# A diffusion step on one Trainium2 core: a fifth unit of the modulation summed on VectorE in the first mixer, begun a quarter of the in-projection earlier, and one narrower widened matmul per head in the second mixer

## The chip, the cores and the metric

The program runs on one core of a Trainium2 chip. The core has a TensorE (matrix products; PE in the profile, its weight loads PEld), a VectorE (DVE), a ScalarE (ACT), a GpSimd (POOL) and a SyncE (SP), which here issues nearly all DMA transfers. Each engine runs its own list of instructions in order, and the engines wait for each other through semaphores. The metric is device time in microseconds (us), as a median of runs; smaller is better.

## What is computed

One step of a diffusion backbone with two layers, for 128 context tokens and 128 latent tokens that share all weights, with D = 2048 features, in 32 bit floating point:

```python
def _trunk(x, cond, rope, caches, w_ada, b_ada, ...):
    for l in range(DEPTH):
        mod = jax.nn.silu(cond) @ w_ada[l] + b_ada[l]
        sh1, sc1, gt1, sh2, sc2, gt2 = jnp.split(mod[:, None, :], 6, axis=-1)
        h = rmsnorm(x, g_norm_mix[l]) * (1 + sc1) + sh1
        ...
            m, new = mixer_ab(h, rope, ctx, w_in_ab[i], ...)
        ...
            m, new = mixer_c(h, rope, ctx, l, w_in_c[i], ...)
        x = x + gt1 * m
        h = rmsnorm(x, g_norm_ffn[l]) * (1 + sc2) + sh2
        x = x + gt2 * conv_ffn(h, w_ffn_up[l], w_ffn_conv[l], b_ffn_conv[l], w_ffn_down[l])
    return rmsnorm(x, g_final), ab_ctx, c_ctx

def mixer_ab(h, rope, ctx, w_in, g_q, w_q_up, g_kv, w_kv_up, g_qn, g_kn, w_out):
    proj = h @ w_in
    ...
    out = jnp.concatenate([out_a.reshape(b, t, -1), out_b.reshape(b, t, -1)], axis=-1) @ w_out
    return out, new_ctx
```

`mixer_ab`, the first mixer, has eight heads of latent attention and eight of grouped attention; `mixer_c`, the second, is differential attention. The modulation `mod` has six vectors of 2048 numbers for each layer and each of the two conditions (`c_ctx` and `c`). Its matrix `w_ada` is 2 x 2048 x 12288 numbers, 201 MB of the 617 MB that the program moves.

## The kernel before

**The products.** Activations stand with features on partitions: `hx[:, k]` holds row k, 128 features by 256 columns (both groups' tokens), as a high half in 256 columns and a low half in the next 256. A weight tile of 1 MB is split into a high part `wh` (ScalarE, L248) and a low part `wl` (VectorE, L249), eight 128 x 128 blocks at a time. Each block then takes three matmuls of 256 columns (L110): high by high, high by low, low by high; I call these three a triplet. `wh` and `wl` have four buffers each, which the splits take in turn. TensorE adds in PSUM into tiles named `acc`.

**The in-projection of the first mixer** runs over 23 chunks (c0 to c22) of 128 output features. It passes over them five times, each time with a part of the 16 rows: `whole` (rows 0, 1), `halves` (2, 3), quarter 1 (rows 4 to 7), quarter 2 (8 to 11) and the last quarter (12 to 15). In the three quarters a chunk takes 12 matmuls. After a chunk VectorE adds its sum to the ones before (L1143). Up to the end of quarter 2, the order of TensorE's instructions is that of the program (`pe.in_turn`); in the rest a scheduler sorts each engine's list by a timeline that it simulates, and `keep_order` holds chosen instructions in the order of the program. What the list then says is fixed: on the chip an engine doesn't run a later instruction first.

**The modulation** is worked out beside these products, in units (l, j, q): layer, vector (0 to 5) and quarter of 512 features. A unit has four tiles of 1 MB (128 x 2048 numbers). There are three ways to make one. A *row unit* (`ROWS`) takes TensorE: 16 matmuls of 32 x 512 for two tiles, a *pair*, and four transposes per unit (L113), then a reduce (L445) and an addition of the bias (L447) on VectorE. A *feature unit* (`FEATS`) is summed on VectorE in the feed-forward layers. A *deep unit* (`DEEP`, class `Deep`) is summed on VectorE in the mixers: each tile comes in two halves of 512 KB (L522), one for each half of the 2048 inputs, and for each half-tile there are two sums, one for each condition (L525; in the trace a custom instruction and a read of its accumulator). A unit has 16 such sums. They need the row `condb` of the conditions, loaded a half (1 MB, L513) at a time and passed through SiLU by ScalarE (L516). `deep.pump` is called after every chunk and takes as many steps as `deep.rate` says, 0.4 a chunk in the last quarter and 1.6 a call in the heads.

**In quarters 1 and 2**, `quarter(q)` says what is done after which chunk: pairs of row units after c4, c8, c13 and c17, the transposes of the first unit after c10, and after c19 those of the second, which complete shift and scale of the next quarter's four rows. Then `rows(q + 1)` calls `modulate`: VectorE scales the four rows (L658, one of the groups) and ScalarE the other group; ScalarE casts the high halves; the low halves come from VectorE for the even rows (L647) and from GpSimd for the odd ones. After c22 the next quarter begins at once with these rows.

**The second mixer** has a matmul with a widened operand at two of 13 places per head, so as to shift the matmuls' rhythm: `PUSH` gives the extra columns. The first is the one that follows the scores, the last the one that follows the head's output.

Of the kernel before, what the change touches and what calls it, by code (L numbers as in the profile page):

```python
# [58 lines left out]

EARLY = (2, 5, 8, 11, 13)  # L60
WIDER = (32, 16, 8, 4, 2)
PUSH = [32] + 11 * [0] + [16]
SENT = (1, 3, 6, 9, 12, 14, 16)
FINE = 4

# [9 lines left out]


ROWS = [(0, j, q) for q in range(4) for j in (1, 0)]
ROWS += [(0, j, q) for j in (2, 4) for q in range(4)]
ROWS += [(0, 5, 0)]
ROWS += [(1, 2, 1), (1, 2, 2), (1, 2, 3), (1, 4, 0), (1, 3, 0)]  # L80
FEATS = [(0, 5, 1), (0, 5, 2), (0, 5, 3)]
FEATS += [(1, j, q) for j in (1, 0) for q in range(4)]
FEATS += [(1, 2, 0)]
FEATS += [(1, 5, q) for q in range(4)]
DEEP = [[(0, 3, q) for q in range(4)], [(1, 4, q) for q in range(1, 4)] + [(1, 3, q) for q in range(1, 4)]]
RLIMIT = {"ab": 16, "ffn0": 17, "c": 22, "ffn1": 22}
FLIMIT = {"ab": 0, "ffn0": 12, "c": 12, "ffn1": 16}

SIDE = {"in3": 0.4, "heads": 1.6, "out0": 1.8, "c": 2.2, "outc": 2.0}
UW = NT + 2  # L90
INV = {2048: 0, 768: 1, 512: 2, 128: 3, 256: 4}

# [2 lines left out]
def step_kernel(ctx: ExitStack, tc: tile.TileContext, A: dict):  # L95
# [96 lines left out]
    def flush():  # L192
        while chains:
            step()
# [299 lines left out]
    class Deep:  # L494
# [50 lines left out]

        def flush(self):
            while self.steps:
                self.step()

    deep = Deep()  # L550
# [366 lines left out]
    def mixer_ab(hx, beside):  # L917
        l = 0
        with tc.tile_pool(name="ab", bufs=1) as ab:
            with tc.tile_pool(name="abp", bufs=1) as pj:  # L920
# [187 lines left out]
                def values(c):  # L1108
                    pt = T_(ppool["att"], [P, 512], "att", bufs=3)
                    for g in range(2):  # L1110
                        pe.transpose(pt[:, g * T:(g + 1) * T], vb[:, c, g * T:(g + 1) * T], ident)
                    act.copy(vg[:, 0, c], pt[:, 0:T])
                    act.copy(vg[:, 2, c], pt[:, T:NT])
                    if c == 1:
                        sp.dma_start(out=A["o_gqa_v"], in_=vg[:, 0])
                    yield

                def finish(c):
                    if c == 7:
                        deep.silu()  # L1120
                        deep.rate = SIDE["in3"]
                    if c < 6:
                        start(queries(c))
                    elif c < 10:
                        start(latents(c - 6))
                    elif c == 10:
                        start(key_rope())
                    elif c < 13:
                        start(keys(c - 11))
                    elif c == 14:  # L1130
                        start(values(0))
                    elif c == 15:
                        start(values(1))
# [60 lines left out]

                def quarter(q):
                    u = 2 * q + 2
                    return {4: lambda: pair(u, 0), 8: lambda: pair(u, 2), 10: turned, 13: lambda: pair(u + 1, 0),
                            17: lambda: pair(u + 1, 2), 19: lambda: turned(q + 1)}

                def at(steps):  # L1200
                    return lambda c: steps[c]() if c in steps else None
# [3 lines left out]
                for q in (1, 2):  # L1205
# [3 lines left out]
                kv_in = T_(ab, [P, 4, 2, 3 * T], "kv_in", F32R)  # L1209
                ql = T_(ab, [P, 6, 2 * NT], "ql", F32R)  # L1210
                caches()
                deep.begin(beside, DEEP[0], [(beside, "block")],
                           mod[:, 0, 5].rearrange("p (i t) c -> p i t c", t=4), hx[:, 0:2])
                deep.cond(0)
                part(rest, 12, 4, False, RATE["in3"], finish)

            with tc.tile_pool(name="abh", bufs=1) as hp:
                ada["pew"] = PEW["heads"]
# [59 lines left out]
                flush()  # L1278
                weigh_lambda()
                start(gqa_query(0))  # L1280
                deep.tiles.append((ab, "kvb"))
                deep.junk = o[:, 6:8]
                deep.rate = SIDE["heads"]
                for h in range(0, 8, 2):
                    for i in range(2):
                        ps = gemm(WQ.chunk(), qh, qlo)
                        qn[h + i] = T_(hp, [P, NT], "qn", bufs=4)
                        act.copy(qn[h + i], ps)
                        pump(RATE["heads"])
                    ps = gemm(WQ.chunk(), qh, qlo)  # L1290
                    ev = T_(tmp, [P, NT], "nt", bufs=4)
                    act.copy(ev, ps)
                    qr = T_(hp, [P, NT], "qr", bufs=2)
                    act.copy(qr[:, 0:T], ev[:, 0:T])
                    rope(qr[:, None, T:], ev[:, None, T:], 1, 32, "rcm", "rsm")
                    pump(RATE["heads"])
                    kn = []
                    for i in range(2):
                        if h + i < 7:
                            start(gqa_query(h + i + 1))  # L1300
                        start(gqa(h + i))
                        ps = gemm(WK.chunk(), kh, klo, 3 * T)
                        kn.append(T_(hp, [P, 3 * T], "kn", bufs=2))
                        act.copy(kn[i], ps)
                        pump(RATE["heads"])
                    mla_pair(h, qr, kn, values())
                flush()

        return o
# [471 lines left out]
```

## Time and profile before

| what | us |
|---|---|
| median of 3 runs (lowest, highest) | 2304.95 (2304.35, 2306.54) |
| the profiled execution | 2307.52 |
| its span | 2305.7 |
| `whole` and `halves` of the in-projection | 26 to 84 |
| quarter 1, quarter 2 | 84 to 126, 126 to 167 |
| last quarter, then the heads (they overlap) | 167 to about 205, to 355 |
| output projection of the first mixer | 355 to 475 |
| first feed-forward layer | 475 to 1166 |
| second mixer with its output projection | 1192 to about 1512 |
| second feed-forward layer | 1580 to 2306 |

All times in views of the profile are microseconds from the start of the span. A row of the timeline gives start, duration, engine, line, operation, the tiles written and read, and, in brackets, idle time before it and what ended that; the recorded durations of neighbours overlap a little, so that the step from one start to the next is the time that one takes in a row of them. In the chain of waits a piece is a stretch on one engine that ended last.

### The profile page before, as it was taken

What the parts mean: (1) busy time and instruction counts of PE and PEld (TensorE: products, weight loads), DVE (VectorE), ACT (ScalarE), POOL (GpSimd) and SP (SyncE); (2) the same over time, 40 slices, a digit from 0 to 9 for tenths busy, and PEclk for the clock granted to TensorE, in tenths of its full rate; (3) what the DMA queues carried; (4) which work ended last, traced back from release to release, by engine and by line L of the source; (5) the groups of instructions that cost most, each with busy time, mean ns of one, the idle gap of its engine ahead of it and who ended that gap; (6) DMA issues with size and microseconds to landing.
All of it is one profiled execution on the core that took longest, in us unless ns stands there. A gap on an engine that the chain in (4) does not pass through costs nothing.

```text
span 2305.7 us, 47484 instructions
## 1 busy us (share of the span) xinstructions
PE 2275.9 (99%) x19496; PEld 2182.1 (95%) x19496; DVE 1885.6 (82%) x2973; ACT 1195.7 (52%) x1959; POOL 188.1 (8%) x238
## 2 busy tenths in 40 slices
PE   8999999999999999999999999999999999999998
PEld 6788878999999999999999999999999999999998
DVE  4667979989999999999978988898899965666654
ACT  4345555665553355555575455457555434555543
POOL 0002111300000000001130001023000000000011
PEclk9999999999999999999999999999999999999999
DMA  9987888777777777777788888776667755555553
GB/s 376 367 343 293 326 311 338 288 277 264 262 255 291 291 272 260 272 258 258 288 293 293 318 322 310 267 268 229 246 256 262 264 200 189 199 191 194 198 189 126
DMA packets 100122, 617.15 MB, mean 268 GB/s; under 512 B 10752, under 2 KB 18880, under 8 KB 33344
## 3 DMA queue, kind: packets, MB, share of 16 engines
q1 hardware_dynamic: 99904, 614.11, 72.2%
q8 instruction: 153, 2.51, 0.4%
q14 instruction: 65, 0.53, 0.1%
HBM read 609.32 MB, written 4.75 MB: 266 GB/s over the span
## 4 chain that ended last, share of the span: by engine, by line
PE 93%; DVE 3%; DMA 2%; issue 1%; POOL 1%; ACT 1%; SPq 0%; DVEq 0%; ACTq 0%; POOLq 0%
PE acc L110 86%; PE ada L110 3%; PE att L110 2%; DVE wl L249 1%; DVE hx L525 1%; DMA more<-w_ada 1%; PE att L113 1%; DMA raw<-w_out_c 0%; PE misc L110 0%; DMA araw<-w_ada 0%; DMA kvb<-w_ada 0%; POOL dev L807 0%; PE ada L113 0%; DVE rope L858 0%; ACT wh L248 0%
## 5 line engine op out<-in xcount | busy, mean ns | idle before, releaser
L110 PE MATMUL acc<-hx,wh 128*128 128x256 f32 (+1 forms) x7264 | 1255.2, 278 | 4.2 <-ACT wh L248 1.7
L248 ACT CAST wh<-raw 128x1024 fp32r<-128x1024 f32 (+1 forms) x834 | 796.6, 967 | 869.8 <-PE acc L110 736.6
L249 DVE TENSOR_TENSOR wl<-raw,wh 128x1024 fp32r<-128x1024 f32 (+1 forms) x834 | 925.4, 1126 | 246.9 <-ACT wh L248 240.2
L110 PEld LDWEIGHTS acc<-hx,wh 128*128 128x128 f32 x7264 | 1099.8, 188 | 23.2 <-ACT wh L248 8.1
L110 PE MATMUL acc<-hx,wl 128*128 128x256 f32 (+1 forms) x3632 | 1007.8, 278 | 5.3 <-DVE wl L249 5.1
L110 PEld LDWEIGHTS acc<-hx,wl 128*128 128x128 f32 x3632 | 684.5, 188 | 9.5 <-DVE wl L249 6.9
L110 PE MATMUL acc<-g,wh 128*128 128x256 f32 x2816 | 478.8, 276 | 0.0
L110 PEld LDWEIGHTS acc<-g,wh 128*128 128x128 f32 x2816 | 424.0, 188 | 0.0
L110 PE MATMUL acc<-g,wl 128*128 128x256 f32 x1408 | 388.1, 276 | 0.0
L473 DVE CUSTOM_DVE_ANT_0 junk<-araw,condb 128x2048 f32<-128x2048 f32 x128 | 294.4, 2300 | 0.0
L110 PEld LDWEIGHTS acc<-g,wl 128*128 128x128 f32 x1408 | 264.2, 188 | 0.0
L211 POOL TENSOR_TENSOR sqacc<-sqacc,sq 128x256 f32<-128x256 f32 x62 | 71.5, 1154 | 1491.1 <-ACT sq L207 1490.9
L110 PE MATMUL acc<-hxc,wh 128*128 128x256 f32 (+1 forms) x1056 | 189.3, 281 | 0.0
L110 PEld LDWEIGHTS acc<-hxc,wh 128*128 128x128 f32 x1056 | 161.9, 188 | 1.8 <-issue 1.7
L110 PE MATMUL acc<-hxc,wl 128*128 128x256 f32 (+1 forms) x528 | 146.9, 278 | 0.0
L110 PEld LDWEIGHTS acc<-hxc,wl 128*128 128x128 f32 x528 | 99.6, 189 | 0.2
L110 PE MATMUL acc<-wh,hxc 128*128 128x256 f32 (+1 forms) x512 | 95.0, 283 | 0.5 <-DVE nt L818 0.5
L1531 ACT ACTIVATE cv<-acc,convw 128x256 f32<-128x256 f32 x169 | 94.1, 557 | 0.0
L525 DVE CUSTOM_DVE_ANT_0 hx<-block,condb 128x1024 fp32r<-128x1024 f32 x65 | 79.3, 1221 | 7.3 <-DMA block<-w_ada 6.8
L1537 DVE SCALAR_TENSOR_TENSOR cv<-acc,convw,cv 128x254 f32<-128x254 f32 x169 | 81.1, 480 | 3.2
L843 DVE SCALAR_TENSOR_TENSOR x<-acc,mod,x 128x128 f32<-128x128 f32 x190 | 57.3, 344 | 31.6 <-PE acc L110 31.6
L110 PEld LDWEIGHTS acc<-wh,hxc 128*128 128x128 f32 x512 | 79.4, 188 | 3.4 <-issue 2.5
(263 smaller groups left out, 1800.4 us busy)
## 6 DMA issues: line engine op xcount, KB each, us to landing
raw<-w_up SPq DMA_DIRECT2D x176, 1024.0 KB, 4.8
araw<-w_ada SPq DMA_DIRECT2D x136, 1024.0 KB, 6.0
raw<-w_down SPq DMA_DIRECT2D x88, 1024.0 KB, 4.8
raw<-w_in_c SPq DMA_DIRECT2D x48, 1024.0 KB, 6.9
block<-w_ada SPq DMA_DIRECT2D x41, 512.0 KB, 6.8
raw<-w_in_ab SPq DMA_DIRECT2D x18, 1024.0 KB, 9.1
raw<-w_out_ab SPq DMA_DIRECT2D x16, 1024.0 KB, 7.9
raw<-w_out_c SPq DMA_DIRECT2D x16, 1024.0 KB, 7.1
```

The costliest lines, as they stand in the source:

```text
L110: return self.placed(nc.tensor.matmul(*a, **kw))
L113: return self.placed(nc.tensor.transpose(*a, **kw))
L211: eng.tensor_tensor(out=st["acc"], in0=st["acc"], in1=sq, op=ALU.add)
L248: pin(act.copy(out_hi, src))
L249: pin(dve.tensor_tensor(out=out_lo, in0=src, in1=out_hi.bitcast(F32), op=ALU.subtract))
L473: keep_order(dve.tensor_tensor_reduce(out=T_(feat["pool"], [P, D], "junk"), in1=feat["row"][:, c], in0=feat["raw"].rearrange("p g n -> p ( ...
L525: keep_order(dve.tensor_tensor_reduce(out=self.junk, in0=self.raw, in1=self.row[:, c].rearrange("p (g n) -> p g n", g=2), scale=1.0, scala ...
L843: dve.scalar_tensor_tensor(out=x[:, c, s], in0=ps[:, s], scalar=mod[:, l, 3 * which + 2, c, g:g + 1], in1=x[:, c, s], op0=ALU.mult, op1=AL ...
L1531: pin(act.activation(y, ps, AF.Identity, scale=cw[:, 1, m:m + 1], bias=cw[:, 3, m:m + 1]))
L1537: pin(dve.scalar_tensor_tensor(out=y3[:, :, :T - 1], in0=p3[:, :, 1:], scalar=cw[:, 2, m:m + 1], in1=y3[:, :, :T - 1], op0=ALU.mult, op1=A ...
```

## The change

`DEEP[0]` gets a fifth unit, (0, 4, 3), which leaves `ROWS`; so the first mixer and the first output projection make seven row units of vectors 2 and 4 where they made eight, and the limits `RLIMIT` fall by one. The deep sums no longer begin in the last quarter but with quarter 1: `begin_sums` loads the first half of `condb` after its chunk c0, `sums_ready` passes it through SiLU after c6 and sets the rate of 0.4. In the in-projection their tiles are `block` and `more` in turn, in the heads `block` and `kvb` as before. `deep.even()` takes a second condition's sum that is still due at the end of the last quarter and of the heads. The first of the two places in `PUSH` gets 16 extra columns instead of 32.

```diff
-PUSH = [32] + 11 * [0] + [16]
+PUSH = [16] + 11 * [0] + [16]
...
-ROWS += [(0, j, q) for j in (2, 4) for q in range(4)]
+ROWS += [(0, j, q) for j in (2, 4) for q in range(4)][:7]
...
-DEEP = [[(0, 3, q) for q in range(4)], [(1, 4, q) for q in range(1, 4)] + [(1, 3, q) for q in range(1, 4)]]
-RLIMIT = {"ab": 16, "ffn0": 17, "c": 22, "ffn1": 22}
+DEEP = [[(0, 4, 3)] + [(0, 3, q) for q in range(4)], [(1, 4, q) for q in range(1, 4)] + [(1, 3, q) for q in range(1, 4)]]
+RLIMIT = {"ab": 15, "ffn0": 16, "c": 21, "ffn1": 21}
...
-SIDE = {"in3": 0.4, "heads": 1.6, "out0": 1.8, "c": 2.2, "outc": 2.0}
+SIDE = {"in": 0.4, "in3": 0.4, "heads": 1.6, "out0": 1.8, "c": 2.2, "outc": 2.0}
...
+        def even(self):
+            while isinstance(self.steps[0], partial) and self.steps[0].func == self.sums and self.steps[0].args[-1]:
                 self.step()
...
                 def finish(c):
-                    if c == 7:
-                        deep.silu()
-                        deep.rate = SIDE["in3"]
...
                 def quarter(q):
                     u = 2 * q + 2
-                    return {4: lambda: pair(u, 0), 8: lambda: pair(u, 2), 10: turned, 13: lambda: pair(u + 1, 0),
-                            17: lambda: pair(u + 1, 2), 19: lambda: turned(q + 1)}
+                    steps = {4: lambda: pair(u, 0), 8: lambda: pair(u, 2), 10: turned, 13: lambda: pair(u + 1, 0),
+                             17: lambda: pair(u + 1, 2), 19: lambda: turned(q + 1)}
+                    return {**steps, 0: begin_sums, 6: sums_ready} if q == 1 else steps
+
+                def begin_sums():
+                    deep.begin(beside, DEEP[0], [(beside, "block"), (pj, "more")],
+                               mod[:, 1, 4:6].rearrange("p j (i t) c -> p (j i) t c", t=4), hx[:, 0:2])
+                    deep.cond(0)
+
+                def sums_ready():
+                    deep.silu()
+                    deep.rate = SIDE["in"]
...
                 caches()
-                deep.begin(beside, DEEP[0], [(beside, "block")],
-                           mod[:, 0, 5].rearrange("p (i t) c -> p i t c", t=4), hx[:, 0:2])
-                deep.cond(0)
+                deep.rate = SIDE["in3"]
                 part(rest, 12, 4, False, RATE["in3"], finish)
+                deep.even()
...
-                deep.tiles.append((ab, "kvb"))
+                deep.tiles = [(beside, "block"), (ab, "kvb")]
...
+                deep.even()
                 flush()
```

Counted over the lists, the sums of the first mixer rise from 64 to 80: in the in-projection, up to the last add of the last quarter, from 2 to 20 (4 in quarter 1, 8 in quarter 2, 8 in the last), in the heads from 44 to 42, in the output projection from 20 to 16. The removed row unit's two pairs and four transposes stood in the output projection. The loads of the caches move from quarter 2 to the last quarter. From the second mixer on TensorE's list is as before, apart from the widths. Lines behind the new `even` have numbers higher by four: L647, L658 and L951 become L651, L662 and L955; L1143 becomes L1144.

What moved on VectorE at the end of quarter 1 (`acc_1222` is chunk c19, the two acc behind it are c20 and c21; `nt_1243` and `nt_1255` are rows 8 and 10 being made), before:

```order
L1143 TENSOR_TENSOR qb_242<-qb_242,acc_1222 128x256
L445 TENSOR_REDUCE mod_77<-ada_1236 128x8
L447 TENSOR_TENSOR mod_77<-mod_77,cst_74 128x8
L658 TENSOR_SCALAR nt_1243<-nt_1243,scl_78,mod_77 128x128
L658 TENSOR_SCALAR nt_1249<-nt_1249,scl_78,mod_77 128x128
L658 TENSOR_SCALAR nt_1255<-nt_1255,scl_78,mod_77 128x128
L658 TENSOR_SCALAR nt_1261<-nt_1261,scl_78,mod_77 128x128
L249 TENSOR_TENSOR wl_1328<-raw_1089,wh_1327 128x1024
L1143 TENSOR_TENSOR qb_242<-qb_242,acc_1281 128x256
L647 TENSOR_TENSOR hx_104<-nt_1243,hx_104 128x256
L1143 TENSOR_TENSOR qb_242<-qb_242,acc_1295 128x256
L647 TENSOR_TENSOR hx_104<-nt_1255,hx_104 128x256
```

And in the change, from the add of chunk c19 (`acc_1236`) on; `nt_1257` is row 8, `raw_1096` and `raw_1175` are the first two weight tiles of quarter 2, `block_1135` a half-tile of a deep unit:

```order
L1144 TENSOR_TENSOR qb_242<-qb_242,acc_1236 128x256
L445 TENSOR_REDUCE mod_77<-ada_1250 128x8
L249 TENSOR_TENSOR wl_1339<-raw_1096,wh_1338 128x1024
L525 ISA hx_104,mod_77<-block_1135,condb_872 128x1024
L525 ISA mod_77 128x1
L447 TENSOR_TENSOR mod_77<-mod_77,cst_74 128x8
L249 TENSOR_TENSOR wl_1343<-raw_1096,wh_1342 128x1024
L1144 TENSOR_TENSOR qb_242<-qb_242,acc_1295 128x256
L1144 TENSOR_TENSOR qb_242<-qb_242,acc_1310 128x256
L525 ISA hx_104,mod_77<-block_1135,condb_872 128x1024
```

```order
L662 TENSOR_SCALAR nt_1275<-nt_1275,scl_78,mod_77 128x128
L1144 TENSOR_TENSOR qb_242<-qb_242,acc_1324 128x256
L249 TENSOR_TENSOR wl_1409<-raw_1175,wh_1408 128x1024
L249 TENSOR_TENSOR wl_1413<-raw_1175,wh_1412 128x1024
L651 TENSOR_TENSOR hx_104<-nt_1257,hx_104 128x256
L651 TENSOR_TENSOR hx_104<-nt_1269,hx_104 128x256
```

Between the two pieces stand the sum's second row and the other three scalings. Ahead of the first, from the add of chunk c17 on, stand a whole and a half weight low of `raw_1030`, the last tile of quarter 1, two sums on `more_1034` and the add of c18. So between the add of c17 and row 8's low half there are now six adds, five whole and one half weight low and four sums. `wh_1412` takes the buffer of `wh_1285`, which chunk c22 of quarter 1 reads, and ScalarE's list has the casts `wh_1408` and `wh_1412` ahead of the cast of row 8's high half.

VectorE at the end of quarter 2, in the change, from the add of c22 (`acc_1806`) on; `nt_1743` and `nt_1755` are rows 12 and 14, `raw_1927` the second weight tile of the last quarter, `acc_1837` its chunk c0:

```order
L1144 TENSOR_TENSOR qb_242<-qb_242,acc_1806 128x256
L651 TENSOR_TENSOR hx_104<-nt_1743,hx_104 128x256
L525 ISA hx_104,mod_77<-more_1658,condb_872 128x1024
L525 ISA mod_77 128x1
L249 TENSOR_TENSOR wl_1930<-raw_1927,wh_1929 128x1024
L525 ISA hx_104,mod_77<-more_1658,condb_872 128x1024
L525 ISA mod_77 128x1
L249 TENSOR_TENSOR wl_1934<-raw_1927,wh_1933 128x1024
L651 TENSOR_TENSOR hx_104<-nt_1755,hx_104 128x256
L1144 TENSOR_TENSOR proj_124<-proj_124,acc_1837 128x256
```

Before, one add stood between the two low halves. Now two sums and two weight lows stand there. From the add of c17 to row 12's low half there are six adds, three whole and one half weight low and two sums (on `block_1565`).

TensorE at the start of the last quarter, in the change; `acc_1837`, `acc_1859` and `acc_1882` are chunks c0, c1 and c2, `wh` and `wl` the parts of the weights; the sixth and the ninth row read row 13, the others row 12:

```order
L110 MATMUL acc_1837<-hx_104,wh_1829 128x256
L110 MATMUL acc_1859<-hx_104,wh_1829 128x256
L110 MATMUL acc_1882<-hx_104,wh_1833 128x256
L110 MATMUL acc_1837<-hx_104,wh_1829 128x256
L110 MATMUL acc_1837<-hx_104,wl_1830 128x256
L110 MATMUL acc_1837<-hx_104,wh_1829 128x256
L110 MATMUL acc_1859<-hx_104,wh_1829 128x256
L110 MATMUL acc_1859<-hx_104,wl_1830 128x256
L110 MATMUL acc_1859<-hx_104,wh_1829 128x256
```

The fourth row is the first that reads a low half of row 12. In the same manner row 13 follows for the three chunks, then row 14's high half for each, and the 22nd matmul is the first that reads row 14's low half. Before, the list here had chunks c0 and c1 in turn.

More of the change, by code (lines that the diff above doesn't have):

```diff
@@ L547, in flush @@
             while self.steps:
+                self.step()
+        def even(self):
+            while isinstance(self.steps[0], partial) and self.steps[0].func == self.sums and self.steps[0].args[-1]:
                 self.step()
```

## The prediction

> **What bounds the kernel now.** I read the chain of waits on the page first, to learn which engine sets the end, then the windows over the first mixer, then the chain and the VectorE timeline at the one place where the change is densest. The span and the chain:
>
> ```profile
> span 2305.7 us, 47484 instructions
> PE 93%; DVE 3%; DMA 2%; issue 1%; POOL 1%; ACT 1%; SPq 0%; DVEq 0%; ACTq 0%; POOLq 0%
> ```
>
> TensorE carries 93% of the chain, so an edit counts by the TensorE work it removes and by the waits it puts ahead of TensorE. The windows (stretch in us; its length, then busy time of PE, PEld, DVE, ACT, POOL; clock; DMA share; GB/s) are: whole and halves, quarter 1, quarter 2, most of the last quarter, the last heads, a piece of these, and the first half of the output projection:
>
> ```profile
> 26.00:84.00 58.00, 51.66 (x425) 41.60 (x425) 33.62 (x84) 27.67 (x58) 0.00 (x0) 0.94 0.97 401
> 84.00:126.00 42.00, 42.00 (x344) 35.73 (x344) 26.74 (x49) 15.42 (x23) 1.63 (x2) 0.96 0.87 350
> 126.00:167.00 41.00, 41.00 (x350) 34.73 (x349) 26.79 (x52) 16.31 (x24) 1.55 (x2) 1.00 0.87 343
> 167.00:205.00 38.00, 38.00 (x312) 32.88 (x312) 30.71 (x67) 25.04 (x54) 10.12 (x12) 1.00 0.73 276
> 300.00:355.00 55.00, 49.23 (x355) 38.41 (x354) 38.44 (x103) 29.03 (x70) 8.88 (x16) 0.94 0.72 277
> 326.00:336.00 10.00, 5.25 (x24) 1.60 (x23) 8.38 (x25) 2.56 (x9) 1.84 (x4) 0.70 0.74 269
> 355.00:415.00 60.00, 59.89 (x511) 53.05 (x509) 58.01 (x106) 32.68 (x58) 11.07 (x10) 1.00 0.94 366
> ```
>
> In both quarters TensorE never idles, and VectorE is idle for 42.00 - 26.74 = 15.3 us and 14.2 us. A share says nothing of order, though: VectorE runs its list strictly, and at a quarter's end that list holds the activation rows with which the next quarter begins.
>
> The chain at the two ends of quarters (start us, us, what):
>
> ```profile
> 116.24 1.85 PE ada L110 x16
> 118.09 2.95 PE acc L110 x24
> 121.48 11.31 PE acc L110 x96
> ...
> 157.42 1.85 PE ada L110 x16
> 159.27 2.95 PE acc L110 x24
> 162.66 14.98 PE acc L110 x132
> ```
>
> Chunk 17 ends at 116.24, a pair of row-unit tiles follows, then chunks 18 and 19, the transposes, and from 121.48 eight chunks without a gap: three of quarter 1 and, from 121.48 + 3/8 x 11.31 = 125.72, quarter 2. There the second matmul needs the low half of row 8, at 125.72 + 11.31/96 = 125.84. VectorE at that time (start, us, operation):
>
> ```profile
> 116.28 0.42 DVE L1143 TENSOR_TENSOR qb<-qb,acc 128x256 f32<-128x256 f32 x1 [0.34 <-PE acc L110]
> ...
> 121.52 0.19 DVE L445 TENSOR_REDUCE mod<-ada 128x8 f32<-128x32 f32 x1
> 121.74 0.17 DVE L447 TENSOR_TENSOR mod<-mod,cst 128x8 f32<-128x8 f32 x1
> 121.95 1.11 DVE L658 TENSOR_SCALAR nt<-nt,scl,mod 128x128 f32<-128x128 f32 x4
> 122.98 1.22 DVE L249 TENSOR_TENSOR wl<-raw,wh 128x1024 fp32r<-128x1024 f32 x1
> 124.11 0.41 DVE L1143 TENSOR_TENSOR qb<-qb,acc 128x256 f32<-128x256 f32 x1
> 124.44 0.86 DVE L647 TENSOR_TENSOR hx<-nt,hx 128x256 fp32r<-128x256 f32 x1
> 125.22 0.41 DVE L1143 TENSOR_TENSOR qb<-qb,acc 128x256 f32<-128x256 f32 x1
> ```
>
> The low half is written from 124.44 and done by 125.22, 0.6 us before TensorE reads it. That is all the slack there is at this place.
>
> **The change part by part.** *The new list at the first boundary.* In the changed order there stand, from chunk 17's add to row 8's low half, six adds, five whole weight lows, half a weight low, four sums, the reduce and bias add, four scalings and the low half itself. Their lengths, as start to next start, come from the rows above and from the heads, where both kinds run back to back:
>
> ```profile
> 234.84 0.68 DVE L249 TENSOR_TENSOR wl<-raw,wh 128x512 fp32r<-128x512 f32 x1
> 235.45 0.18 DVE L445 TENSOR_REDUCE mod<-ada 128x8 f32<-128x32 f32 x1
> ...
> 238.23 1.22 DVE L249 TENSOR_TENSOR wl<-raw,wh 128x1024 fp32r<-128x1024 f32 x1
> 239.37 1.22 DVE L525 CUSTOM_DVE_ANT_0 hx<-block,condb 128x1024 fp32r<-128x1024 f32 x1
> 240.51 0.08 DVE L525 DVE_READ_ACCUMULATOR2_ANT mod<- 128x1 f32 x1
> ```
>
> A weight low takes 239.37 - 238.23 = 1.14, a sum 1.14, a half low 0.61, an add 124.44 - 124.11 = 0.33, reduce and bias 121.95 - 121.52 = 0.43, the scalings 1.03, the low half 0.4 (an add's size). So 6 x 0.33 + 5 x 1.14 + 0.61 + 4 x 1.14 + 0.43 + 1.03 + 0.4 = 14.7 us: from 116.28 to 131.0, against 125.84. **TensorE waits 5.2 us.** Queued behind it on VectorE are only row 10's low half and the next lows; the chunks that use those lows are themselves held back by row 8.
>
> The low end has a reason of its own. The last weight low ahead of row 8 needs a buffer that chunk 22 reads to its end at 125.72, and ScalarE's cast before it:
>
> ```profile
> L248 ACT CAST wh<-raw 128x1024 fp32r<-128x1024 f32 (+1 forms) x834 | 796.6, 967 | 869.8 <-PE acc L110 736.6
> ```
>
> 125.72 + 0.97 + 1.14 + 0.4 = 128.2, so 2.4 us are lost however early the sums run. At the high end I put two sums more, 7.5, for tiles that land late. I take 5.2, as the list has no gap in it.
>
> *The second boundary.* Chunk 17 ends at 157.42 and chunk 22 at 162.66 + 3/11 x 14.98 = 166.75. Here TensorE's changed order interleaves the first three chunks of the last quarter: its fourth matmul needs row 12's low half (167.09), its 22nd row 14's (169.13). On VectorE, row 12's comes after six adds, three and a half lows, two sums and the row's own work: 2.0 + 3.4 + 0.6 + 2.3 + 0.4 + 1.0 + 0.4 = 10.1 from 157.45, or 167.55. Row 14's comes two sums, two lows and itself later, 5.0, so at 172.5. **TensorE waits 172.5 - 169.1 = 3.4 us.** The floor, by the same buffer, is 166.75 + 0.97 + 1.14 + 0.4 = 169.3, 0.2 us; the high end 5.7.
>
> *The last quarter and the DMAs.* VectorE gets four sums more in 167 to 205, 4.6 us into 38.00 - 30.71 = 7.3 us of idle time, and the caches' loads move there. Quarter 1 moves 350 x 42 = 14.7 MB; half of the condition row and three half-tiles add 2.5. At the 401 GB/s of the first window 42 us hold 16.8 MB. I take +1 for both together (0 to 4.6). [...]
>
> *The clock.* A wait of this size already occurs once between 84 and 475, in the heads:
>
> ```profile
> PE att L113 <- DVE p L904: 4.5, 1, 4.5
> ```
>
> The window 326:336 around it shows clock 0.70, that is 3.0 us' worth of clock lost in 10, of which some fell in the wait itself; in the window TensorE was busy for 5.25 us and idle for 4.75. So one such wait costs from 0 (no fall) to 3.0. The 5.2 us wait may bring it once; the 3.4 us one is shorter than the 4.5 that did, and in two parts of 0.5 and 2.9: +2 for both (0 to 6). [...]
>
> *The row unit.* It goes from the output projection:
>
> ```profile
> 389.20 1.85 PE ada L110 x16
> 391.06 17.16 PE acc L110 x144
> 408.21 1.85 PE ada L110 x16
> 415.73 0.44 PE ada L113 x4
> ```
>
> These 2 x 1.85 + 0.44 = **4.1 us** of TensorE are on the chain and leave it whole. VectorE takes them over as 16 sums. In the output projection its sums fall from 20 to 16, which relieves a VectorE that is busy for 58.01 of 60. TensorE is idle there for only 0.11 us, but between the two pairs its matmuls go at 17.16/48 = 0.357 us a triplet, where 0.340 occurs elsewhere (below): -0.5 for these 48, and from 0 to -2.8 if some 200 of such triplets gain as the rows of the push show. In the heads the sums go from 44 to 42 and end a little earlier; TensorE idles for 55.00 - 49.23 = 5.8 us there, so -5 to +5 with 0 taken.
>
> *The push.* In the second mixer, of a head's two widened matmuls the first narrows:
>
> ```profile
> 1238.59 0.48 PE L110 MATMUL acc<-wh,hxc 128*128 128x288 f32 x1
> 1238.91 0.28 PE L110 MATMUL acc<-wl,hxc 128*128 128x256 f32 x1
> ...
> 1240.32 0.28 PE L110 MATMUL acc<-wl,hxc 128*128 128x256 f32 x1
> ...
> 1242.32 0.41 PE L110 MATMUL acc<-hxc,wh 128*128 128x272 f32 x2
> 1242.57 0.28 PE L110 MATMUL acc<-hxc,wl 128*128 128x256 f32 x1
> ...
> 1243.93 0.28 PE L110 MATMUL acc<-hxc,wl 128*128 128x256 f32 x1
> ```
>
> After the 288 wide one four triplets take 1240.32 - 1238.91 = 1.41 us, after the 272 wide one 1243.93 - 1242.57 = 1.36: 0.0125 us a triplet. If 16 columns switch the pace at both places, the ten triplets between them in each of eight heads gain 8 x 10 x 0.0125 = 1.0 us; if they leave it in the wrong one past the second place, as much again or more is lost. I take -0.3 (-1.6 to +3).
>
> *Sum:* 5.2 + 3.4 + 1 + 2 - 4.1 - 0.5 + 0 - 0.3 = **+6.7 us**. The profiled execution took 2307.52 (span 2305.7 and 1.8 around it), which becomes 2314.2; against the median of the runs, 2304.95, it is **2311.7**.
>
> **The rivals.** *A, the forecast*, +6.7: the sums stand in front of the rows. For it speaks that VectorE is strict and that the slack was 0.6 us; against it, that I derive the start of the list (no delay from earlier) from before.
>
> *B, VectorE is not the limit at the boundaries* (not slower): the sums ahead of the turn run in the 15.3 us that VectorE idles in a quarter, and only the buffers' floors remain, 2.4 + 0.2. No wait is long enough to pull the clock down, and VectorE's relief in the output projection then counts whole: 2.6 - 4.1 - 2.8 - 0.3 = -4.6, or 2300.3. It decides if the four sums ahead of row 8 are finished by 126.7, when the last weight low can start. Against it: two of the four stand behind lows of tiles that TensorE needs only in quarter 2.
>
> *C, only the first boundary is late:* by the interleaved chunks the second costs its floor, and the clock stays: 5.2 + 0.2 + 1 - 4.9 = +1.5, or 2306.5. It decides if row 14's low half is written by 169.3.
>
> *D, the heads suffer as well:* with the turn of the two tiles shifted a sum waits for its tile ahead of a head's softmax, as before the 4.5 us wait, and one such wait with its clock is added, 4.5 + 2.5: +13.7, or 2318.7. For it: that wait exists once already. Against it: two sums fewer there.
>
> **How the numbers follow.** Chances: A 0.54, B 0.26, C 0.10, D 0.10. What a measurement of this kernel can tell from no change is about 0.2%, 4.6 us: below 2300.3 is faster, above 2309.6 slower. B lies on the lower bound and its open costs (the push, the heads) lean to a gain, so 0.17 of it counts faster and 0.09 same. C gives 0.02 faster, 0.06 same, 0.02 slower. A gives 0.49 slower, 0.04 same (with no fall of the clock and a boundary near its floor) and 0.01 faster (with 5 us back in the heads). D is slower. Together faster 0.20, same 0.19, slower 0.61. A's own range is 2307 to 2318: clock 0 to 6, boundaries each 1.5 to either side, the last quarter 0 to 4.6, the heads 2 to either side, combined as independent. The range that should hold 8 in 10 reaches to B with half the push, 2299, and to D with its clock, 2321.
>
> **What would show it.** In the profile after: TensorE idle near 126 for about 5 us and near 167 to 172 for about 3, both put down to VectorE's row lows (L651); the stretch 84 to 205 longer by 9 to 12 us; a clock below 1.00 just after the first wait; the output projection shorter by 4 to 5; the span from the feed-forward on equal within 2 us. No gap at 126 over 3 us refutes A. A second mixer that changes by more than 3 us shows the push mis-sized. A gap that is put down to a DMA shows that the tiles, not VectorE's list, were late.

## The result: slower by one per cent, and the profile after

| | us |
|---|---|
| before, median of 4 runs | 2305.05 (2304.35 to 2306.54) |
| changed, median of 4 runs | 2327.93 (2325.44 to 2330.02) |
| ratio, with its 95% interval | 1.0098 (1.008 to 1.0115) |
| profiled executions and their spans | 2307.52 and 2305.7; 2330.02 and 2328.2 |

The forecast was 2311.7 and a range to 2321. The direction came as forecast, the size was more than three times as large: +22.9 us instead of +6.7. In the profiles, each of one execution, the growth is 2330.02 - 2307.52 = 22.5 us.

To see where the time went, I take the start of the same instruction in both traces, at seven places, and the growth of the distance from one place to the next. All runs that follow are read in the same way; the table is worked out from single starts in the traces. (Column 1: from the start of the span to quarter 1's last row-unit pair, 116.2 before. 2: to quarter 2's third pair, 149.6. 3: to the in-projection's last add, 210.4. 4: to the second head's first exponential, 230.3. 5: to the first residual add, 356.2. 6: to an operation inside the first feed-forward, 603.6. 7: to the beginning of the second feed-forward, about 1594; behind that no kernel moves by more than 0.5 us.)

| kernel | 1 start | 2 first boundary | 3 second boundary, last quarter | 4 heads' start | 5 other heads | 6 output projection | 7 rest |
|---|---|---|---|---|---|---|---|
| the change | -1.7 | +7.5 | +4.7 | **+15.5** | +0.2 | -3.1 | -0.9 |
| e1, push 32 | -2.1 | +8.1 | +6.8 | +14.6 | -0.8 | -1.9 | -0.9 |
| e2, heads' list in program order | -0.1 | +7.3 | +5.1 | +6.4 | -0.1 | -3.6 | -0.8 |
| e3, sums in mid quarter 2 | -1.4 | +3.5 | +6.2 | +3.0 | -2.7 | +14.2 | -0.8 |
| e4, stop after chunk 9 | -2.8 | +4.5 | +4.4 | -0.5 | +3.2 | +10.1 | -0.9 |
| e5, held before the heads | -0.4 | +7.6 | +6.2 | +2.6 | -0.8 | -3.5 | -0.9 |
| e6, middle of the parts | -0.9 | +5.3 | +10.2 | +3.1 | -2.3 | -2.4 | -0.3 |
| e7, the same, 1.8 in the heads | -2.9 | +6.2 | +12.4 | +2.9 | +5.0 | -4.0 | -0.8 |
| e8, five units begun late | -3.0 | 0.0 | 0.0 | +9.2 | -0.9 | +26.7 | -0.4 |
| e9, first pair of heads held | +1.6 | +7.7 | +6.7 | +7.8 | +7.0 | -1.2 | -0.6 |
| e10, two ahead | -0.8 | +6.2 | +5.1 | +5.1 | -1.8 | +1.8 | -0.6 |
| e11, none ahead of row 8 | -1.0 | +6.8 | +7.9 | +7.4 | +0.8 | -2.1 | -0.5 |
| e12, before with push 16 | -1.5 | -0.1 | 0.0 | -0.4 | +0.6 | 0.0 | +0.8 |

Column 1 differs by some us between kernels with the same instructions there; it is no effect of an edit. A row is one execution, within 2.5 us of its kernel's median, except that e9's is 6.5 us above and e4's 3.5 us below it.

**The first boundary** is as the list said. VectorE in the change (start, us):

```profile
116.08 1.22 DVE L525 CUSTOM_DVE_ANT_0 hx<-more,condb 128x1024 fp32r<-128x1024 f32 x1
...
118.38 1.22 DVE L525 CUSTOM_DVE_ANT_0 hx<-more,condb 128x1024 fp32r<-128x1024 f32 x1
...
121.09 1.22 DVE L525 CUSTOM_DVE_ANT_0 hx<-block,condb 128x1024 fp32r<-128x1024 f32 x1
...
124.11 1.22 DVE L525 CUSTOM_DVE_ANT_0 hx<-block,condb 128x1024 fp32r<-128x1024 f32 x1
...
126.62 2.35 DVE L249 TENSOR_TENSOR wl<-raw,wh 128x1024 fp32r<-128x1024 f32 x2
128.89 0.76 DVE L651 TENSOR_TENSOR hx<-nt,hx 128x256 fp32r<-128x256 f32 x2
```

There are the four sums, then the last two weight lows, then the row lows at 128.89. TensorE beside it, at both boundaries:

```profile
126.33 0.38 PE L110 MATMUL acc<-hx,wh 128*128 128x256 f32 x1 [2.41 <-ACT hx L666]
129.36 0.58 PE L110 MATMUL acc<-hx,wh 128*128 128x256 f32 x1 [2.65 <-DVE hx L651]
```

```profile
173.22 0.84 PE L110 MATMUL acc<-hx,wh 128*128 128x256 f32 x4 [0.67 <-ACT hx L666]
175.42 0.38 PE L110 MATMUL acc<-hx,wh 128*128 128x256 f32 x1 [0.43 <-POOL hx L651]
179.67 0.38 PE L110 MATMUL acc<-hx,wh 128*128 128x256 f32 x1 [2.94 <-DVE hx L651]
```

The brackets give the waits: 2.41 + 2.65 = 5.1 us, and 4.0 us. The first 2.41 us are put down to ScalarE's cast of row 8's high half, not to VectorE's low half. They too begin on VectorE: ScalarE's scaling of the rows, which stands ahead of that cast, waited for the bias addition (L447), and this came behind three of the four sums.

```profile
122.44 1.65 ACT L665 ACTIVATE nt<-nt,mod,scl 128x128 f32<-128x128 f32 x4 [2.10 <-DVE mod L447]
```

What ends the whole wait is row 8's low half at 129.23.

**The start of the heads** is the new place, and the largest. The windows of 10 us there (columns as before), in the change and, for the same work, before:

```profile
220.00:230.00 10.00, 10.00 (x87) 8.55 (x87) 9.81 (x23) 5.55 (x10) 0.48 (x1) 1.00 0.84 306
230.00:240.00 10.00, 7.07 (x39) 5.07 (x38) 5.23 (x17) 3.24 (x8) 4.70 (x11) 0.80 0.98 369
240.00:250.00 10.00, 9.17 (x36) 7.38 (x37) 9.64 (x25) 4.80 (x13) 6.08 (x8) 0.52 0.83 299
```

```profile
215.00:225.00 10.00, 10.00 (x73) 7.59 (x66) 7.06 (x20) 3.13 (x9) 2.50 (x4) 1.00 0.92 317
225.00:235.00 10.00, 10.00 (x85) 8.95 (x84) 8.33 (x24) 7.73 (x20) 3.10 (x7) 1.00 0.95 388
```

Between 230 and 250 TensorE gets through 75 matmuls where before it does 158 in as long, and its clock is 0.80 and 0.52. In these 20 us it is idle for 3.8. Its 16.2 busy us would have taken about 7.07 x 0.80 + 9.17 x 0.52 = 10.4 at a clock of 1.00 (an estimate), so the clock, which falls among these short waits, loses 5.8, more than the waits themselves. VectorE's list tells why TensorE waits. Each query of a head is rotated by VectorE (L864, L865 in the change) before TensorE can form that head's scores. From the last add (220.90) on, the sums and the first two rotated queries are:

```profile
223.14 1.22 DVE L525 CUSTOM_DVE_ANT_0 hx<-more,condb 128x1024 fp32r<-128x1024 f32 x1
...
231.38 1.22 DVE L525 CUSTOM_DVE_ANT_0 hx<-block,condb 128x1024 fp32r<-128x1024 f32 x1
232.52 0.08 DVE L525 DVE_READ_ACCUMULATOR2_ANT mod<- 128x1 f32 x1
232.52 0.29 DVE L865 TENSOR_TENSOR qb<-qb,rope 128x128 f32<-128x128 f32 x1
...
247.72 1.22 DVE L525 CUSTOM_DVE_ANT_0 hx<-block,condb 128x1024 fp32r<-128x1024 f32 x1
249.18 0.29 DVE L865 TENSOR_TENSOR qb<-qb,rope 128x128 f32<-128x128 f32 x1
```

Four sums stand ahead of the first rotated query and ten ahead of the second, which is done at 249.5, 28.6 us after the last add. Before, none and two stood there (219.62 and 220.88), and the second was done at 225.7, 15.3 us after the last add:

```profile
210.44 0.41 DVE L1143 TENSOR_TENSOR qb<-qb,acc 128x256 f32<-128x256 f32 x1
...
216.57 0.29 DVE L861 TENSOR_TENSOR qb<-qb,rope 128x128 f32<-128x128 f32 x1
219.62 1.23 DVE L525 CUSTOM_DVE_ANT_0 hx<-block,condb 128x1024 fp32r<-128x1024 f32 x1 [2.76 <-DMA block<-w_ada]
...
225.43 0.29 DVE L861 TENSOR_TENSOR qb<-qb,rope 128x128 f32<-128x128 f32 x1
```

Before, the tiles were loaded too late to stand in the way: VectorE even waited 2.76 us for the first. In the change two tiles, `more` and `block`, are in place from the last quarter: their first sum, at 223.14, begins without a wait. TensorE's list in the change goes along with it: between two pieces of the second key projection it has seven queries' statistics (short matmuls, `misc`; the expectations below speak of five) and a row-unit pair, and no projection.

```profile
234.93 0.58 PE L110 MATMUL misc<-cst,sq 128*128 128x1 f32 x4 [1.03 <-ACT qb L1241]
236.58 1.94 PE L110 MATMUL ada<-araw,condw 128*32 128x512 f32 x8 [1.07 <-DMA araw<-w_ada]
...
239.88 0.99 PE L110 MATMUL misc<-cst,sq 128*128 128x1 f32 x4 [0.41 <-DVE rv L219]
...
245.45 1.01 PE L110 MATMUL acc<-kv_in,wh 128*128 128x384 f32 x2
```

The projection at 245.45 then runs without a wait: it was there to be done, only further back in the list.

### The profile page after: what moved, and what is told of

The parts are those of the page before. It is cut to its first block, busy times and chain, and to the rows that moved or that the text cites. A ratio compares the mean times of both kernels' runs of the same rounds, so it can differ in the third digit from the quotient of the medians.

```text
span 2328.2 us, 47463 instructions
## 1 busy us (share of the span) xinstructions
PE 2282.2 (98%) x19460; PEld 2189.7 (94%) x19460; DVE 1906.0 (82%) x3005; ACT 1195.4 (51%) x1958; POOL 193.4 (8%) x238
## 4 chain that ended last, share of the span: by engine, by line
PE 91%; DVE 5%; DMA 2%; issue 1%; ACT 1%; POOL 1%; SPq 0%; DVEq 0%; ACTq 0%; POOLq 0%
PE acc L110 85%; PE ada L110 3%; PE att L110 2%; DVE wl L249 1%; DVE hx L525 1%; DMA araw<-w_ada 1%; DMA raw<-w_in_ab 1%; DVE u L525 1%; PE att L113 1%; POOL dev L811 0%; PE ada L113 0%; DMA block<-w_ada 0%; PE misc L110 0%; DVE x L847 0%; ACT wh L248 0%
## 5 line engine op out<-in xcount | busy, mean ns | idle before, releaser
L525 DVE CUSTOM_DVE_ANT_0 hx<-block,condb 128x1024 fp32r<-128x1024 f32 x71 | 86.7, 1221 | 4.6 <-DMA block<-w_ada 4.2
```

The source lines that it names most:

```text
L525: keep_order(dve.tensor_tensor_reduce(out=self.junk, in0=self.raw, in1=self.row[:, c].rearrange("p (g n) -> p g n", g=2), scale=1.0, scala ...
```

## The experiments

All ratios are to before, on the same chip, with 95% intervals.

**The push: e1 and e12.** In e1 the change gets the old push, in e12 before gets the new one.

```diff
-PUSH = [16] + 11 * [0] + [16]
+PUSH = [32] + 11 * [0] + [16]
```

> The change with the push of 32 columns put back, all else as changed. In the two profiles the second mixer's milestones keep the same distance within 0.4 us up to the sixth head. Theory (the push is worth less than 2 us here): 2326 to 2330, the second mixer within 2 us of the changed one. Rival (the narrower push costs several us): 2324 or less.

> Before with the narrower push alone. In the change and in the run with 32 columns put back, the second mixer kept its distance from before within 0.1 us of each other, so: 2304 to 2306, no difference (under 1 us in the second mixer of the profiles). Rival (the push gains only where the pace ahead of it is that of before): 2302 or less.

e1: 2331.03 us, 1.0112 (1.0096 to 1.0129), so a little above the upper end expected; the difference from the change lies in columns 1 to 6, ahead of any push, and column 7, which holds the second mixer, is -0.9 in both. e12: 2305.27 us over 10 runs, 1.000 (0.999 to 1.001). The push is worth nothing that these runs can tell: in the second mixer, the 512 matmuls `acc<-wh,hxc` take 286.2 us from the first start to the last before, in the change and in e1, and 286.4 in e12. The -0.9 that the change shows behind the feed-forward stands with either push.

**The order of TensorE's list in the heads: e2.** `pe.in_turn` holds TensorE's instructions of the first pair of heads in program order; VectorE's sums ahead of the second query stay ten.

```diff
                 for h in range(0, 8, 2):
+                    pe.in_turn = h == 0
...
-                    mla_pair(h, qr, kn, values())
+                    vm = values()
+                    pe.in_turn = False
+                    mla_pair(h, qr, kn, vm)
```

> The change, with TensorE's instructions of the first head pair held in program order; sums, tiles and loads are the same, and the list up to the heads is the same. Theory L (the 15 us lost between 211 and 256 come from the order of TensorE's list there: five heads' statistics and a row unit's pair without a projection between them): at least 8 us come back, 2316 to 2320, both boundary waits stay (5 us near 126, 4 us near 171). Rival Q (the row unit's tiles come late because the sums' tiles crowd the queue): any order waits, 2325 to 2331, with a wait of over 2 us for araw near 230.

2322.20 us, 1.0073 (1.0058 to 1.0088), between the ranges of L and Q. Column 4 falls from 15.5 to 6.4, so the arrangement of the list costs 9 us, but L is not the whole; and the wait of over 2 us for `araw` that Q wanted is not there. What remains is a wait for VectorE:

```profile
246.44 1.22 PE L110 MATMUL att<-kg,qb 128*128 128x256 f32 x2 [7.48 <-DVE qb L865]
```

The second head's scores wait 7.48 us for the query behind ten sums.

**No sums ahead of the rows: e3 and e4.** `hold` sets the rate to 0, `resume` sets it to `SIDE["in"]`. e3 has no sums in quarter 1 and a rate of 0.8 in quarter 2; e4, 0.8 in both. The diff shows e4; in e3 the first of the two returned lines has `6: deep.silu, 21: hold` in place of `6: sums_ready, 9: hold`.

```diff
-                    return {**steps, 0: begin_sums, 6: sums_ready} if q == 1 else steps
+                    if q == 1:
+                        return {**steps, 0: begin_sums, 6: sums_ready, 9: hold}
+                    return {**steps, 1: resume, 9: hold}
```

> The change without sums in quarter 1, and in quarter 2 only from chunk 1 to chunk 9 at a rate of 0.8, so that none stands ahead of the rows at either boundary; the condition row is still loaded and prepared in quarter 1; 11 sums in the in-projection where there were 20, the rest later. Theory S (the sums ahead of the rows make the boundary waits): TensorE waits at most 2.5 us at the first boundary and 1 at the second; together with a list in the heads that has projections between the statistics: 2300 to 2309. Rival (the waits come from the tiles' and the condition row's transfers): the waits stay over 4 us. If L is wrong, the loss between 211 and 256 stays and the time is 2314 or more.

> The change with the rate raised to 0.8 and the sums stopped after chunk 9 of quarters 1 and 2: 2 and 6 sums there, 8 in the last quarter. None stands between chunk 17's add and the rows, but four whole weight lows still do at the first boundary. Theory S: the first wait falls from 5.1 to 0.5 to 2.5 us, the second from 4 to under 1.5; with L 2301 to 2311. Rival: the waits stay over 4 us.

Both missed in the total: 2329.77 us, 1.0105 (1.009 to 1.012), and 2329.44 us, 1.0105 (1.0088 to 1.0121). At the first boundary they did about what theory S says. e3 waits 1.75 us there, and e4:

```profile
123.12 0.39 PE L110 MATMUL acc<-hx,wh 128*128 128x256 f32 x1 [0.32 <-ACT hx L666]
125.35 0.48 PE L110 MATMUL acc<-hx,wh 128*128 128x256 f32 x1 [1.84 <-DVE hx L651]
127.36 0.58 PE L110 MATMUL acc<-hx,wh 128*128 128x256 f32 x1 [0.46 <-DVE hx L651]
```

That is 2.6 us, a little over the 0.5 to 2.5 expected. At the second boundary both wait 1.9 us (in e3 0.94 + 0.77 + 0.15), more than the 1 and 1.5 that theory S allowed, but far from the rival's 4; most of it is put down to VectorE's adds (L1144), which stand behind two weight lows and the split of a cache. So the sums ahead of the rows account for 2.5 to 3.4 of the 5.1 us and for 2.1 of the 4.0, not for all of them. The heads' start costs 3.0 and -0.5, with five and two sums ahead of the second query. What came back was lost at the end of the output projection, column 6: 26 and 23 sums stood there instead of 16, the last of them behind all 32 residual adds, where in the change six of the 32 follow the last sum. TensorE's waits from 430 to 500 in e3 (us, times, longest):

```profile
PE acc L110 <- ACT u L726: 11.5, 1, 11.5
```

L726 copies the shift of the feed-forward's rows, which the last deep units make.

**The heads' start alone: e5.** Quarters 1 and 2 as in the change; in the last quarter the sums go faster and stop before the heads.

```diff
-SIDE = {"in": 0.4, "in3": 0.4, ...
+SIDE = {"in": 0.4, "in3": 0.6, ...
                 def finish(c):
+                    if c == 13:
+                        deep.rate = 0.0
```

> The change, but in the last quarter the sums go at a rate of 0.6 and are held from chunk 13 on, so that one sum instead of ten stands on VectorE between the end of the in-projection and the second head's rotated query; quarters 1 and 2 are as in the change, 39 sums in the heads, 18 in the output projection (16 in the change). Theory V (the 15 us lost at the start of the heads come from sums ahead of the first heads' queries on VectorE, which TensorE's list only follows): from the end of the in-projection to the first residual add the time is that of before within 5 us, in all 2312 to 2319. Rival (fifth unit's loads on the queues, or the order of TensorE's list alone): 2323 to 2330. Both boundary waits stay (5 and 4 us).

2319.28 us, 1.0062 (1.0047 to 1.0077), 0.3 us over what V expected and well below the rival's range. The boundary waits are those of the change (2.43 + 2.65 us at the first), and column 4 falls from 15.5 to 2.6:

```profile
223.91 0.41 DVE L1146 TENSOR_TENSOR qb<-qb,acc 128x256 f32<-128x256 f32 x1
224.24 1.22 DVE L525 CUSTOM_DVE_ANT_0 hx<-block,condb 128x1024 fp32r<-128x1024 f32 x1
...
236.16 0.29 DVE L865 TENSOR_TENSOR qb<-qb,rope 128x128 f32<-128x128 f32 x1
239.41 1.23 DVE L525 CUSTOM_DVE_ANT_0 hx<-kvb,condb 128x1024 fp32r<-128x1024 f32 x1 [1.94 <-DMA kvb<-w_ada]
```

One sum stands ahead of the second query, which is done 12.5 us after the last add, and the windows from 225 to 255 show TensorE busy for 29.63 of 30 us at clock 1.00. TensorE's list changed with it, since the scheduler made it from the same timeline: no row of statistics any more. 13 of the 15.5 us are so shown to come from the sums ahead of the queries, by both ways: VectorE itself (6.4 in e2), and the list that the scheduler made around them.

**Held in the first pair of heads: e9.**

```diff
-                deep.rate = SIDE["heads"]
                 for h in range(0, 8, 2):
+                    deep.rate = 0.0 if h == 0 else 2.1
```

> The change with no sums begun during the first pair of heads and a rate of 2.1 after it: 6 sums instead of 10 ahead of the second head's rotated query, all of them from tiles that the last quarter had begun; TensorE's list there still has five heads' statistics in a row, as in the change. Theory V in its plain form (each sum ahead of the queries costs about its 1.2 us): 4 to 6 us come back, 2321 to 2325. If TensorE's list alone makes the loss: 2326 to 2331.

2330.17 us, 1.0112 (1.0093 to 1.0131). The total lies in the range of the rival (the list alone), but not for its reason: the list kept its row of statistics, and column 4 still gave back 7.7 us for four sums fewer, more than V's plain price. The other heads, with the higher rate, then lost 7.0 us.

**The fifth unit begun late: e8.**

```diff
-                    return {**steps, 0: begin_sums, 6: sums_ready} if q == 1 else steps
+                    return steps
...
                 def finish(c):
+                    if c == 7:
+                        sums_ready()
...
-                deep.rate = SIDE["in3"]
+                begin_sums()
```

> Five units, but begun in the last quarter, as the four were before: the in-projection's list is that of before, 2 sums there, 44 in the heads, 34 in the output projection, where 20 were. Theory (what isn't summed early is paid at the end of the output projection, where the next layer's rows wait for the last unit): no boundary wait, within 5 us of before up to the first residual add, then a wait of 8 to 20 us near 450: 2312 to 2325. Rival (only the early begin costs, VectorE has room for a fifth unit): 2299 to 2305.

2341.70 us, 1.0157 (1.0142 to 1.0172): more than even the theory expected, since here too six sums stand ahead of the second query (column 4, +9.2, in which TensorE waits 1.66 us for VectorE and also 1.67 us for a row unit's tile) and the output projection loses 26.7. There TensorE's waits, and two windows of 15 us, are:

```profile
PE acc L110 <- ACT u L726: 19.6, 2, 12.3
```

```profile
445.00:460.00 15.00, 3.76 (x16) 2.96 (x16) 14.10 (x32) 7.92 (x21) 9.95 (x13) 0.54 0.54 181
460.00:475.00 15.00, 2.67 (x12) 2.21 (x12) 13.35 (x30) 5.60 (x17) 9.66 (x11) 0.50 0.21 70
```

TensorE stands almost still while VectorE works off its sums. It also shows that the loss in the in-projection is the early begin's own: 0.0 in columns 2 and 3.

**Other places for the sums: e6, e7, e10, e11.** All start from the edits of e4 and e5 together, with the stops and rates that the expectations name; in e7 the sums of quarter 2 also resume one chunk later than in e6.

> The sums run in the middle of the parts: in quarter 1 at 0.8 until chunk 9, in quarter 2 at 1.2 from chunk 1 to 9, in the last at 0.8 until chunk 13; 2, 9 and 11 sums there, 38 in the heads, 20 in the output projection, as many as before. At the first boundary no sum and four weight lows stand ahead of row 8, at the second two sums and one low; one sum ahead of the second head's query. Theories S and V together: first wait 2 to 3 us, second under 1, the heads within 5 us of before, the row unit's 4 us kept: 2302 to 2311. If more sums in the output projection's last part are what costs (as in the run with 11 sums in the in-projection, which waited 11.5 us there), a wait of over 3 us near 450 and 2312 or more.

> As the run with the sums in the middle, with 0.7 in the last quarter and 1.8 in the heads: 2, 8, 9 sums in the in-projection, 46 in the heads, 15 in the output projection. If the end of the output projection is the limit, faster than that run by 1 to 4 us: 2299 to 2308; if VectorE in the heads is the limit, slower by 2 to 6: 2306 to 2315.

> Sums held from chunk 11 on in quarters 1 and 2 (rates 0.8 and 0.9) and from chunk 13 on in the last (0.6): 4, 8 and 8 sums as in the change, but two instead of four ahead of row 8, two and one weight low instead of two and three ahead of row 12, two ahead of the second head's query as before; 22 in the output projection. By the arithmetic of the list the first wait is 5.1 - 2 x 1.14 = 2.8 us, the second under 1; heads within 3 us of before; the end of the output projection 0 to 4 us. In all 2304 to 2313.

> Sums held from chunk 9 in quarter 1, 12 in quarter 2 and 13 in the last (rates 0.8, 0.7, 0.7; heads 1.7): 2, 8 and 8 sums, none ahead of row 8 (four weight lows), one sum and one low ahead of row 12, six ahead of the second head's query; 20 in the output projection, done as early as in the change. First wait 2.5, second under 1, heads 3 to 7 us over before, row unit's 4 us kept: 2304 to 2313. Under 2304 it beats before.

All four missed, on the slow side: 2321.44 us, 1.0071 (1.0054 to 1.0088); 2326.02, 1.0091 (1.0076 to 1.0106); 2323.59, 1.008 (1.0065 to 1.0095); 2327.70, 1.0098 (1.0083 to 1.0113). In e6 the output projection's end stayed free, as it should with 20 sums, but the last quarter lost 10.2, with waits for weight casts (4.2 us between 84 and 190, ScalarE) and weight lows. e7 waited 4.0 us for a row unit's tile in quarter 2, behind the sums' tiles. In e10 the first wait was 2.5 + 1.6 = 4.1 us, not the 2.8 of the list, which here has gaps: VectorE idles for 0.94 and 0.16 us in it, waiting for chunks 19 and 20. e11 lost 7.4 at the heads' start with six sums there, as expected, but 6.8 in column 2 with none ahead of row 8; that is more than the 4.5 of e4 mainly by the clock: the waits are 3.1 us for e4's 2.6, but the clock's losses, added up over windows of 2 us, are 3.4 us for e4's 1.7. None of the arrangements tried beat before; the best five-unit kernel is e5.

Over the runs, column 4 against the sums ahead of the second rotated query: ten, 15.5 (14.6 in e1), or 6.4 with the list in program order; six, 7.8, 7.4 and 9.2; five, 3.0; one or two, -0.5 to 5.1. Before has two.

## Why the prediction was right and wrong

*The boundaries* were right. The list was worked out to take 14.7 us; in the trace it goes from 114.61 to 129.23, without a gap. The waits are 5.1 and 4.0 us for 5.2 and 3.4, though 2.41 of the first and 0.67 of the second are put down to ScalarE and not to the row lows that I had named. At the second boundary a weight low and a sum took 1.76 us each instead of 1.2, both overlapping GpSimd's own row lows (173.56 to 175.37, 176.06 to 177.06); the same rows in e5 show the same. What made them longer is not shown: at the first boundary two weight lows beside GpSimd's row lows took 128.89 - 126.62 = 2.27 us, 1.14 each. Rivals B and C are out by these waits. The floors fared less well. At the first boundary e4's 2.6 us agree with 2.4 in size only: the cast ahead of its last weight low before row 8 starts at 121.73, before chunk 22 ends at 122.8, and so didn't wait for the buffer. No run shows the reason that I gave. At the second, 1.9 us stayed in e3 and e4 where I had a floor of 0.2.

*The clock* after the first wait was right in size: column 2 is 7.5 for 5.1 of waiting, beside +2, and the windows of 2 us from 128 to 134 show a clock of 0.50, 0.50 and 0.61. That the second wait added nothing to this (1.00 in the change behind 2.94 us) was luck: the same wait brought the clock down in e1 (0.50), e5 and e9 (last section). *The last quarter*: 4.7 in column 3 for 3.4 + 1. *The row unit*: column 6 is -3.1 for -4.6, and -1.2 to -4.0 in the other runs with at most 20 sums there. *The push*: 0 for -0.3.

*The heads* are the step that failed: "In the heads the sums go from 44 to 42 and end a little earlier ... with 0 taken". The count itself was the wrong way round, here and in the section on the change (the lists have 2 + 42 + 20 = 64 sums before and 20 + 44 + 16 = 80 in the change), but the larger fault is that I counted a stage and not a place. I had listed what stands ahead of the rows at two boundaries, and did not do so at the third place where a part begins with small operations of VectorE, the first heads' queries. There ten sums stand where two stood, and it cost 15.5 us, more than all other terms together. The bounds of -5 to +5 were taken from TensorE's idle time in another stretch of the heads and had no tie to this list.

Rival D had the place and the sign, at 7 us, but the wrong mechanism: the sums did not wait for their tiles; the tiles were there early, and before they had been late enough to do no harm. The other columns add up to +6.7 (+8.4 without the start's -1.7, which is no effect), beside the +6.7 of the forecast; that the two sums meet is chance.

B's premise that none of its waits, 2.4 us at the most, is long enough to pull the clock down was an estimate that no run shows: in e3 the clock was at 0.50 behind a wait of 1.75 us (last section).

## What to carry to other kernels

The engines here ran their lists in order (row 8's low half, at 128.89, came behind everything that stands ahead of it in VectorE's list). Such an engine has room where its list has a gap, not where its busy share is low: at every place where a part of the program begins with short operations of that engine, list what now stands ahead of them, all of those places, before costing anything. Work that is ready early is put early; a load that came late may have been what kept it out of the way. And when each way of placing the same extra work moves the loss to another place (here boundaries, heads' start, heads, the end of the output projection), that speaks for an engine that is full. It does not prove it: eleven arrangements with the fifth unit were tried, and none came out ahead of before.

## What the runs showed of the hardware that I had not expected

In e3 a wait much shorter than those that I had priced was followed by a fall of the clock. TensorE, busy without a gap up to 125.12, waits 1.75 us; windows of 2 us:

```profile
126.00:128.00 2.00, 1.13 (x6) 1.14 (x7) 2.00 (x4) 0.00 (x0) 0.00 (x0) 0.78 1.01 426
128.00:130.00 2.00, 2.00 (x11) 2.00 (x11) 0.94 (x3) 0.00 (x0) 0.00 (x0) 0.50 1.02 430
130.00:132.00 2.00, 2.00 (x17) 2.00 (x16) 0.42 (x1) 1.05 (x1) 0.00 (x0) 0.86 0.79 324
```

The clock is at half for some 3 us behind the wait, which so costs about as much again as it lasted: (0.22 + 0.50 + 0.14) x 2 = 1.7 us. But the 2.94 us wait at the change's second boundary, up to 179.67, left the clock at 1.00. In e1, whose list is the same there, a wait of 2.94 us up to 179.9 brought it to half. The change, then e1:

```profile
180.00:184.00 4.00, 4.00 (x38) 4.00 (x37) 3.16 (x6) 3.00 (x7) 0.85 (x1) 1.00 0.86 300
```

```profile
180.00:182.00 2.00, 2.00 (x10) 2.00 (x11) 0.42 (x1) 0.00 (x0) 0.00 (x0) 0.50 0.94 287
182.00:184.00 2.00, 2.00 (x11) 2.00 (x11) 0.94 (x3) 1.80 (x4) 0.00 (x0) 0.50 0.89 356
```

e2 went as the change, e5 and e9 as e1, and their column 3 is 1.5 to 2.1 us larger than the change's. So the length of a wait alone does not decide, and one trace shows one of two outcomes; what decides, no run here shows. Among the short waits from 232 to 243 in the change the clock fell as well: it is 0.50 in every window of 2 us from 236 to 248, although no single wait there exceeds 1.1 us.
